# A decoder layer's FFN by two-by-two products: loads a pair ahead, half tiles, another order of products and splits, and state loads issued by SP

## The chip, the cores and the metric

The kernel runs on one core of one Trainium2 chip. The metric is the device time of one execution in microseconds (us), as the median of the runs shown. An execution's profile gives a span, from its first to its last instruction, and the granted clock of TensorE (PE). The other engines are VectorE (DVE), ScalarE (ACT), GpSimd (POOL) and SyncE (SP), which here only issues transfers.

## The reference

One inference step of one decoder layer, for 512 prompt rows and 8 sample rows (520 columns once transposed). The parts that the change touches are the second half of the FFN and the sample group's recurrent states (`step`, for 8 samples of 32 heads, 64 by 128 each):

```python
    def step(h, inp):
        st, dec = inp
        return h * dec[..., None, None] + st, h
...
x = x + g1 * mix
h2 = rmsnorm(x, norm2_w) * (1 + sc2) + sh2
gt, up = jnp.split(h2 @ w_ffn_in, 2, axis=-1)
x = x + g2 * ((jax.nn.silu(gt) * up) @ w_ffn_out)
return x, pool_new, conv_new, ssm_new.astype(ssm_prev.dtype)
```

`w_ffn_in` is 1024 x 5632: 22 column tiles of 128 for the gate, 22 for the up part. `w_ffn_out` is 2816 x 1024: 8 output columns of 128, each over 22 tiles of 128 rows. Everything is float32. Each operand is split into a rounded part (`hi`) and the rest (`lo`), and a product is three matmuls: hi by hi, hi by lo, lo by hi.

## The kernel before

**Splits.** A weight tile is loaded by SP as `raw` (three buffers, `NRAW`), cast by ACT to `hi` (L117 or L157) and subtracted by DVE to `lo` (L118 or L158). `hi` and `lo` tiles have three buffers each, so a new cast waits until PE is done with the third tile before it.

**The FFN's first half.** Tiles 0 to 2, 20 and 21 are plain (`ffn`, L1433): two columns of 48 matmuls, then Silu on ACT and a product on DVE (L1393, L1394). Tiles 3 to 19 are 17 "pairs" (`wino`, L1527): the gate's and the up part's tile of one index are taken as a two-by-two block matrix (a11, a12 from the gate tile, a21, a22 from the up tile, each four k blocks deep), and the activations as another; seven products of 12 matmuls replace eight. `sums_of_rows` (L1455) forms once the four sums of activations that the pairs need (t0 to t3, on DVE and POOL) and splits them into `tt`. For every pair POOL forms four sums of weight blocks in place in `raw` (L1511 to L1514: a22, a21, a11, a12, each needing the one before it). They and the original blocks are split into the tiles g (both halves of the gate tile), x, y and z. Seven products go to PSUM in the order g0, g1, y0, x1, y1, z, x0; ACT copies the first (L1546), and DVE adds the others into `u2`, `u4`, `va`, `vb`, `sa`, `sb` (L1545). Silu (L1558) and a product (L1562) end the pair. PSUM has four single banks for these products, so the fifth waits until the first is read out.

**Order of the work around the change.** From `ffn_act` (L1310) on PE, ACT, DVE, POOL and SP work through the program in the order in which it is written: each engine takes its next instruction and waits for what that needs. In pair j the gate's split for pair j+1 (`wino_weights`, L1485) is written after the second product, the sums and the other splits (`wino_sums`, L1500) after the seventh, and the load of pair j+2's tiles (`wino_load`, L1477) after those.

**The FFN's second half and the states.** `ffn_out` (L1615) computes six output columns of 22 k blocks; a column's weights are three units of 8, 8 and 6 k blocks. `ahead` (L170) writes, ahead of a column, the splits of its own third unit and of the first two units of the next column. At five points of each column `states_step` (L1367) takes a step of `sample_states` (L1341), 32 states in all: POOL issues the loads of state n+2 (`hs`, four buffers, L1337; a broadcast row `bb`, three buffers, L1338), multiplies `hs` by its decay (L1353), ACT forms four scaled rows (L1359), and one step later DVE adds them (L1362) and POOL issues the store to `out_ssms` (L1363). So POOL's order in step n is: load n+2, multiply n, store n-1. `last_pair` (L1654) computes the last two output columns, and `finish` normalizes and stores the result.

Of the kernel before, what the change touches and what calls it, by code (L numbers as in the profile page):

```python
# [53 lines left out]
def tile_decoder(ctx: ExitStack, tc: tile.TileContext, I: dict, O: dict):  # L54
# [1275 lines left out]
    def state_load(n):  # L1330
        if n >= 32:
            return
        g, b = state_unit(n)
# [3 lines left out]
        nc.gpsimd.dma_start(out=h, in_=I["sssm"][g, :, b : b + 2])  # L1337
        nc.gpsimd.dma_start(out=bb, in_=dbc[g, 0, b : b + 2].unsqueeze(0).broadcast_to([P, 2, P]))  # L1338
        states[n] = h, bb

    def sample_states():  # L1341
# [4 lines left out]
        before = None
        for n in range(33):
            if n < 32:
                g, b = state_unit(n)
# [3 lines left out]
                nc.gpsimd.tensor_tensor(h, h, at.unsqueeze(3).broadcast_to([P, 2, 2, P]), ALU.mult)  # L1353
                t = G["ff"].tile([P, T], F32, tag="fs", name=f"ht{n}", bufs=NFS)[:, 0:TP]
                t = t.rearrange("p (b j n) -> p b j n", b=2, j=2)
                for i in range(2):
                    for j in range(2):
                        x = xds[:, 2 * g + j, b + i : b + i + 1]
                        nc.scalar.activation(t[:, i, j], bb[:, i], AF.Identity, bias=0.0, scale=x)  # L1359
            if before:  # L1360
                pg, pb_, ph, pt = before
                nc.vector.tensor_tensor(ph, ph, pt, ALU.add)  # L1362
                nc.gpsimd.dma_start(out=O["ssms"][pg, :, pb_ : pb_ + 2], in_=ph)  # L1363
            before = (g, b, h, t)
            yield True
# [89 lines left out]
    def sums_of_rows():  # L1455
        v, p = nc.vector.tensor_tensor, nc.gpsimd.tensor_tensor
        add, minus = ALU.add, ALU.subtract
        for k in range(4):
            b = [[[hblock(n, r, c)[:, k].bitcast(F32) for c in range(2)] for r in range(2)] for n in ("hh", "hl")]
            f1, f2 = (G["ff"].tile([P, T], F32, tag="fs", name=f"ft{k}_{i}", bufs=NFS) for i in range(2))  # L1460
            t1, t2, t3, t4 = f1[:, 0:H2], f1[:, H2:T], f2[:, 0:H2], f2[:, H2:T]
            p(t3, b[0][1][1], b[0][0][1], minus)
            p(t3, t3, b[1][1][1], add)
            p(t3, t3, b[1][0][1], minus)
# [12 lines left out]
    def wino_load(j):  # L1477
        if WINO[0] <= j < WINO[1]:
            WW["raw", j] = load(I["wfi"][j]), load(I["wfi"][NF + j])

    def wino_tiles(j, kind):
        pool, bufs = (wp, 3) if kind in "gz" else (G["we"], 2 if kind == "x" else 1)
        hi, lo = (("hi", "lo") if kind in "gz" else (f"{kind}hi", f"{kind}lo"))
        WW[kind, j] = [pool.tile([P, KD, P], F32R, tag=t, name=f"w{kind}{t}{j}", bufs=bufs) for t in (hi, lo)]

    def wino_weights(j):

        if not WINO[0] <= j < WINO[1]:
            return
        if ("raw", j) not in WW:  # L1490
            wino_load(j)
        g, u = WW["raw", j]
        wino_tiles(j, "g")
        hi, lo = WW["g", j]
        nc.scalar.copy(hi, g)
        nc.vector.tensor_tensor(lo, g, hi.bitcast(F32), ALU.subtract)
        wino_tiles(j, "x")
        split(*(t[:, 0:4] for t in WW["x", j]), u[:, 4:8])

    def wino_sums(j, between=lambda: None, silu=lambda: None):  # L1500

        if not WINO[0] <= j < WINO[1]:
            silu()
            between()
            return
        g, u = WW.pop(("raw", j))
        a11, a12, a21, a22 = g[:, 0:4], g[:, 4:8], u[:, 0:4], u[:, 4:8]
        wino_tiles(j, "y")
        wino_tiles(j, "z")
        v = nc.gpsimd.tensor_tensor  # L1510
        v(a22, a21, a22, ALU.add)  # L1511
        v(a21, a11, a21, ALU.subtract)  # L1512
        v(a11, a22, a11, ALU.subtract)  # L1513
        v(a12, a12, a11, ALU.subtract)  # L1514
        cuts = [("x", 1, a22), ("y", 0, a11), ("z", 0, a12), ("y", 1, a21)]
        cuts = [(*(t[:, 4 * h : 4 * h + 4] for t in WW[n, j]), a) for n, h, a in cuts]
        for hi, lo, a in cuts[:2]:
            nc.scalar.copy(hi, a)
        silu()
        for hi, lo, a in cuts[:2]:  # L1520
            nc.vector.tensor_tensor(lo, a, hi.bitcast(F32), ALU.subtract)
        between()
        for hi, lo, a in cuts[2:]:
            split(hi, lo, a)
        wino_load(j + 1)

    def wino(j):  # L1527
        def fn():
# [7 lines left out]
            def mult(kind, half, x):  # L1536
# [9 lines left out]
            nc.scalar.copy(u2, mult("g", 0, B(0, 0)))  # L1546
            add(sa, mult("g", 1, B(1, 0)), u2)
            wino_weights(j + 1)
            add(u2, mult("y", 0, tt[1]), u2)
            add(u4, mult("x", 1, tt[0]), u2)  # L1550
            o = mult("y", 1, tt[2])
            add(vb, o, u4)
            add(va, o, u2)
            add(sb, mult("z", 0, B(1, 1)), u4)
            o = mult("x", 0, tt[3])

            def silu():
                nc.scalar.activation(s, s, AF.Silu, bias=0.0, scale=1.0)  # L1558

            def between():  # L1560
                add(va, o, va)
                nc.vector.tensor_tensor(s, f2, s, ALU.mult)  # L1562

            wino_sums(j + 1, between, silu)
            for kind in "gxyz":
# [234 lines left out]
```

## Time and profile before

| | us |
|---|---|
| runs | 1215.45, 1215.19, 1212.05 (median 1215.19) |
| the profiled execution | 1213.03 |
| its span | 1211.3 |
| PE busy in it | 1083.4 |
| mean granted PE clock | 0.958 |

A timeline row reads: start, duration, engine, line, operation, output <- inputs with their sizes, count, and in brackets the idle time of the engine before it and what ended that. A row of the waits reads: who waited for whom, us in total, times, longest. PE's rows show a matmul's whole latency; two that follow each other start one matmul's pace apart.

### The profile page before, as it was taken

How to read it: one execution, taken by the hardware profiler on the slowest of the kernel's cores; microseconds unless marked ns; L12 is line 12 of the kernel's file. 1: busy time of each engine (PE TensorE's matmuls, PEld its weight loads, DVE VectorE, ACT ScalarE, POOL GpSimd, SP SyncE). 2: the span in 40 equal slices, each digit the busy share in tenths (PEclk: the TensorE clock that was granted, in tenths of full speed). 3: DMA queues.
4: the chain of work that ended last, by engine and by line, in shares of the span. 5: the costliest groups of instructions: out<-in, count | busy, mean ns of one | idle time of the engine just before them, and what ended most of it. 6: DMA issues, size and time to landing. Idle time of an engine off the chain costs nothing.

```text
span 1211.3 us, 22506 instructions
## 1 busy us (share of the span) xinstructions
PE 1083.4 (89%) x9127; PEld 1041.0 (86%) x9127; DVE 793.2 (65%) x1226; ACT 543.5 (45%) x1003; POOL 355.2 (29%) x514
## 2 busy tenths in 40 slices
PE   7988999999999999999999996888888899666685
PEld 6987999999999999999999976787777889666675
DVE  5686787777877978966765547676676682333342
ACT  4358466556644457543433342333333363334330
POOL 1132423433343310000000142434433412445451
PEclk9998999999999999999999998999999999877787
DMA  9542554346335244544445320222122144555552
GB/s 361 192 118 90 166 175 144 101 154 191 101 118 183 86 140 161 165 140 139 158 140 203 130 105 35 71 80 95 70 79 96 71 149 128 168 157 172 175 174 80
DMA packets 58472, 165.36 MB, mean 137 GB/s; under 512 B 10881, under 2 KB 16513, under 8 KB 57601
## 3 DMA queue, kind: packets, MB, share of 16 engines
q1 hardware_dynamic: 51712, 142.96, 35.5%
q0 software_dynamic: 6656, 20.98, 5.5%
q8 instruction: 71, 1.16, 0.4%
q14 instruction: 33, 0.26, 0.1%
HBM read 151.05 MB, written 12.86 MB: 135 GB/s over the span
## 4 chain that ended last, share of the span: by engine, by line
PE 54%; DMA 15%; POOL 12%; DVE 7%; issue 6%; ACT 5%; SPq 0%; POOLq 0%; DVEq 0%; ACTq 0%
PE m L130 45%; DMA out_ssms<-hs 7%; DMA raw<-in_wfi 5%; POOL hs L1353 2%; POOL raw L1513 2%; PE b L130 2%; DMA araw<-in_wad 2%; POOL raw L1512 2%; POOL raw L1511 2%; PE b L796 1%; POOL hs L1337 1%; PE b L771 1%; POOL bb L1338 1%; PE b L798 1%; DVE wxxlo L158 1%
## 5 line engine op out<-in xcount | busy, mean ns | idle before, releaser
L130 PE MATMUL m<-hh,whi 128*128 128x260 f32 (+1 forms) x1296 | 271.9, 289 | 4.7 <-ACT v L645 3.4
L130 PE MATMUL m<-hh,wlo 128*128 128x260 f32 (+1 forms) x1296 | 265.1, 284 | 1.1 <-DVE wlo L118 1.0
L130 PE MATMUL m<-hl,whi 128*128 128x260 f32 (+1 forms) x1296 | 265.1, 284 | 0.6 <-DVE hl L158 0.2
L130 PEld LDWEIGHTS m<-hh,whi 128*128 128x128 f32 x1296 | 202.5, 190 | 11.0 <-ACT v L645 3.6
L118 DVE TENSOR_TENSOR wlo<-raw,whi 128x1024 fp32r<-128x1024 f32 (+1 forms) x132 | 163.6, 1249 | 70.3 <-ACT whi L117 69.7
L130 PEld LDWEIGHTS m<-hh,wlo 128*128 128x128 f32 x1296 | 202.4, 190 | 1.5 <-DVE wlo L118 1.5
L130 PEld LDWEIGHTS m<-hl,whi 128*128 128x128 f32 x1296 | 202.2, 190 | 1.3 <-DVE hl L158 0.8
L117 ACT CAST whi<-raw 128x1024 fp32r<-128x1024 f32 (+1 forms) x132 | 133.2, 1020 | 137.0 <-PE m L130 107.8
L653 DVE SCALAR_TENSOR_TENSOR v<-xb,cwh,v 128x512 f32<-128x512 f32 x96 | 72.0, 751 | 39.4 <-POOL xb L640 19.3
L130 PE MATMUL m<-ah,whi 128*128 128x260 f32 x264 | 58.3, 305 | 39.3 <-ACT whi L117 39.3
L342 POOL TENSOR_TENSOR r<-me,mhalf 128x5 f32<-128x5 f32 (+2 forms) x6 | 6.4, 1068 | 259.0 <-DVE me L341 259.0
L1362 DVE TENSOR_TENSOR hs<-hs,ht 128x512 f32<-128x512 f32 x32 | 22.8, 712 | 91.0 <-POOL hs L1353 90.9
L130 PEld LDWEIGHTS m<-ah,whi 128*128 128x128 f32 x264 | 45.4, 210 | 40.3 <-ACT whi L117 40.3
L1359 ACT ACTIVATE ht<-bb,xds 128x128 f32<-128x128 f32 x128 | 40.8, 390 | 68.9 <-DMA bb<-dbc 68.8
L130 PE MATMUL m<-ah,wlo 128*128 128x260 f32 x264 | 58.3, 305 | 3.5 <-DVE wlo L118 3.5
L1511 POOL TENSOR_TENSOR raw<-raw 128x512 f32<-128x512 f32 x17 | 21.8, 1285 | 126.4 <-DVE wxxlo L158 126.4
L130 PE MATMUL m<-al,whi 128*128 128x260 f32 x264 | 57.4, 302 | 0.0
L644 ACT COPY xb<-m 128x520 f32<-128x520 f32 (+1 forms) x31 | 17.9, 577 | 81.0 <-PE m L130 81.0
L130 PE MATMUL m<-gh,whi 128*128 128x260 f32 x256 | 52.8, 288 | 0.0
L130 PE MATMUL m<-gl,whi 128*128 128x260 f32 x256 | 51.3, 282 | 0.0
L130 PE MATMUL m<-gh,wlo 128*128 128x260 f32 x256 | 51.3, 282 | 0.0
L130 PEld LDWEIGHTS m<-ah,wlo 128*128 128x128 f32 x264 | 45.1, 209 | 4.9 <-DVE wlo L118 4.9
(383 smaller groups left out, 2757.3 us busy)
## 6 DMA issues: line engine op xcount, KB each, us to landing
raw<-in_win SPq DMA_DIRECT2D x73, 512.0 KB, 4.8
raw<-in_wfi SPq DMA_DIRECT2D x44, 512.0 KB, 4.1
araw<-in_wada SPq DMA_DIRECT2D x24, 512.0 KB, 4.0
h<-in_sssm SPq DMA_DIRECT2D x16, 512.0 KB, 4.2
raw<-in_wssd SPq DMA_DIRECT2D x16, 512.0 KB, 3.4
hs<-in_sssm POOLq DMA_DIRECT2D x32, 256.0 KB, 3.3
raw<-in_wfo SPq DMA_DIRECT2D x16, 512.0 KB, 5.2
out_ssms<-hs POOLq DMA_DIRECT2D x32, 256.0 KB, 2.8
```

Of the source, the lines that this page charges most:

```text
L117: nc.scalar.copy(hi, raw)
L118: nc.vector.tensor_tensor(lo, raw, hi.bitcast(F32), ALU.subtract)
L130: nc.tensor.matmul(o, a[:, k, c0 : c0 + P], b[:, t0:t1], start=f, stop=e)
L158: nc.vector.tensor_tensor(lo, src, hi.bitcast(F32), ALU.subtract)
L644: nc.scalar.copy(shape(xb[:, 3 + t0 : 3 + t1]), o)
L653: nc.vector.scalar_tensor_tensor(v[:, 0:TP], xb[:, k : k + TP], w(k), v[:, 0:TP], ALU.mult, ALU.add)
L1353: nc.gpsimd.tensor_tensor(h, h, at.unsqueeze(3).broadcast_to([P, 2, 2, P]), ALU.mult)
L1359: nc.scalar.activation(t[:, i, j], bb[:, i], AF.Identity, bias=0.0, scale=x)
L1362: nc.vector.tensor_tensor(ph, ph, pt, ALU.add)
L1511: v(a22, a21, a22, ALU.add)
L1512: v(a21, a11, a21, ALU.subtract)
L1513: v(a11, a22, a11, ALU.subtract)
```

## The change

- `sums_of_rows` stands before tile 1's `ffn` instead of after it. It works on two k blocks at a time (two rounds of 520-wide operations instead of four of 260), in buffers of `as` that are not yet in use, and the last-but-one sum (t4, two operations a round) moves from DVE to POOL.
- Loads run two pairs ahead: `wino_load(j + 2)` is written in pair j after the second product, and odd pairs put the up tile into a buffer of its own (`ur`).
- The half tiles x0, x1, y0, y1 get a rotation of five buffers. The products go in the order g0, g1, x0, y0, x1, y1, z.
- A pair begins with the next pair's first splits: x0, then POOL's sums a22 and a21; then the Silu and product left over from the pair before; then the gate tile's split and POOL's a11 and a12. The splits y0, x1, z and y1 stand between the adds of the products.
- `state_load` issues from SP. A state's add and store stand in its own step. The last two of the six columns take six steps (`STEPS`), so that no state is left over.

```diff
-        nc.gpsimd.dma_start(out=h, in_=I["sssm"][g, :, b : b + 2])
-        nc.gpsimd.dma_start(out=bb, in_=dbc[g, 0, b : b + 2].unsqueeze(0).broadcast_to([P, 2, P]))
+        nc.sync.dma_start(out=h, in_=I["sssm"][g, :, b : b + 2])
+        nc.sync.dma_start(out=bb, in_=dbc[g, 0, b : b + 2].unsqueeze(0).broadcast_to([P, 2, P]))
...
-            if before:
-                pg, pb_, ph, pt = before
-                nc.vector.tensor_tensor(ph, ph, pt, ALU.add)
-                nc.gpsimd.dma_start(out=O["ssms"][pg, :, pb_ : pb_ + 2], in_=ph)
-            before = (g, b, h, t)
+            nc.vector.tensor_tensor(h, h, t, ALU.add)
+            nc.gpsimd.dma_start(out=O["ssms"][g, :, b : b + 2], in_=h)
...
+    def wino_first(n, mult=None, silu=None):
+        if WINO[0] <= n < WINO[1]:
+            g, u = WW["raw", n]
+            a11, a12, a21, a22 = g[:, 0:4], g[:, 4:8], u[:, 0:4], u[:, 4:8]
+            split(*half_tile(n, "x0"), a22)
+            v = nc.gpsimd.tensor_tensor
+            v(a22, a21, a22, ALU.add)
+            v(a21, a11, a21, ALU.subtract)
+        if silu:
+            silu()
+            mult()
+        if WINO[0] <= n < WINO[1]:
...
+            split(hi, lo, g)
+            v(a11, a22, a11, ALU.subtract)
+            v(a12, a12, a11, ALU.subtract)
...
+            wino_first(j + 1, *G.pop("left", ()))
+            nc.scalar.copy(u2, mult("g", B(0, 0)))
+            add(sa, mult("g", B(1, 0), 1), u2)
+            wino_load(j + 2)
+            p4 = mult("x0", tt[3])
+            p6 = mult("y0", tt[1])
+            wino_cut(j + 1, "y0")
+            add(u2, p6, u2)
+            add(va, p4, u2)
+            p5 = mult("x1", tt[0])
+            wino_cut(j + 1, "x1", "z")
+            add(u4, p5, u2)
+            p7 = mult("y1", tt[2])
+            wino_cut(j + 1, "y1")
+            add(vb, p7, u4)
+            add(va, p7, va)
...
+            add(sb, mult("z", B(1, 1)), u4)
...
+    todo(sums_of_rows)
     for j in range(1, W0):
...
-        if j == 1:
-            todo(sums_of_rows)
```

On ACT, around the row sums, before: the two casts of tile 2's weights (`whi`), then tile 1's Silu, then the casts of the row sums (`t0h` and on; `ft` holds a sum).

```order
L117 CAST whi_9051<-raw_9049 128x1024
L117 CAST whi_9057<-raw_9055 128x1024
L1393 ACTIVATE as_8976<-m_9061 128x520
L157 CAST t0h<-ft_0_9161 128x260
L157 CAST t1h<-ft_0_9161 128x260
L157 CAST t3h<-ft_1_9162 128x260
```

After the change (`as_8985` and on hold the sums):

```order
L158 CAST t0h<-as_8985 128x520
L158 CAST t1h<-as_8986 128x520
L158 CAST t3h<-as_8988 128x520
L158 CAST t2h<-as_8987 128x520
L158 CAST t0h<-as_8989 128x520
L158 CAST t1h<-as_8990 128x520
L158 CAST t3h<-as_8992 128x520
L158 CAST t2h<-as_8991 128x520
L118 CAST whi_9087<-raw_9085 128x1024
L118 CAST whi_9093<-raw_9091 128x1024
```

All eight casts of row sums now stand ahead of the casts of tile 2's weights. On DVE the subtractions moved in the same way.

On DVE, one pair before, from the gate's split of the next pair to its last half tile (`wxx`, `wyy`, `wz`, `wg` are the tiles x, y, z, g; `fs` and `as` the sums of products; `b` a PSUM bank):

```order
L1496 TENSOR_TENSOR wglo_9935<-raw_9900,wghi_9934 128x1024
L158 TENSOR_TENSOR wxxlo_9939<-raw_9902,wxxhi_9938 128x512
L1545 TENSOR_TENSOR fs_0_9904<-b_9942,fs_0_9904 128x260
L1545 TENSOR_TENSOR fs_0_9904<-b_9956,fs_0_9904 128x260
L1545 TENSOR_TENSOR fs_1_9905<-b_9970,fs_0_9904 128x260 x2
L1545 TENSOR_TENSOR as_8982<-b_9985,fs_0_9904 128x260
L1521 TENSOR_TENSOR wxxlo_9939<-raw_9902,wxxhi_9938 128x512
L1521 TENSOR_TENSOR wyylo_10013<-raw_9900,wyyhi_10012 128x512
L1545 TENSOR_TENSOR fs_1_9905<-b_9999,fs_1_9905 128x260
L1562 TENSOR_TENSOR as_8982<-fs_1_9905,as_8982 128x520
L158 TENSOR_TENSOR wzlo_10015<-raw_9900,wzhi_10014 128x512
L158 TENSOR_TENSOR wyylo_10013<-raw_9902,wyyhi_10012 128x512
```

One pair after, from the first split of the next pair (`wx0el`) to the add of the sixth product (`ur` and `raw` are the loaded tiles):

```order
L159 TENSOR_TENSOR wx0el_10016<-ur_9922,wx0eh_10015 128x512
L1553 TENSOR_TENSOR as_8982<-fs_1_9879,as_8982 128x520
L159 TENSOR_TENSOR wglo_10024<-raw_9924,wghi_10023 128x1024
L1532 TENSOR_TENSOR as_8983<-b_10043,fs_0_10013 128x260
L159 TENSOR_TENSOR wy0el_10088<-raw_9924,wy0eh_10087 128x512
L1532 TENSOR_TENSOR fs_0_10013<-b_10074,fs_0_10013 128x260
L1532 TENSOR_TENSOR fs_1_10014<-b_10061,fs_0_10013 128x260
L159 TENSOR_TENSOR wx1el_10107<-ur_9922,wx1eh_10106 128x512
L159 TENSOR_TENSOR wzlo_10111<-raw_9924,wzhi_10110 128x512
L1532 TENSOR_TENSOR fs_0_10013<-b_10093,fs_0_10013 128x260
L159 TENSOR_TENSOR wy1el_10129<-ur_9922,wy1eh_10128 128x512
L1532 TENSOR_TENSOR fs_1_10014<-b_10115,fs_0_10013 128x260
```

The splits were in two groups around the adds, and now stand one or two at a time between them; the pair's closing product (L1553) stands after the next pair's x0 split.

On POOL, two steps of the states before:

```order
L1353 TENSOR_TENSOR hs_12104<-hs_12104,dtx 128x512
L1363 DMA out_ssms<-hs_12068 128x512
L1337 DMA hs_12250<-in_sssm 128x512
L1338 DMA bb_12251<-dbc 128x256
L1353 TENSOR_TENSOR hs_12178<-hs_12178,dtx 128x512
L1363 DMA out_ssms<-hs_12104 128x512
L1337 DMA hs_12286<-in_sssm 128x512
L1338 DMA bb_12287<-dbc 128x256
```

After, three steps on POOL:

```order
L1360 DMA out_ssms<-hs_11978 128x512
L1352 TENSOR_TENSOR hs_11982<-hs_11982,dtx 128x512
L1360 DMA out_ssms<-hs_11982 128x512
L1352 TENSOR_TENSOR hs_11986<-hs_11986,dtx 128x512
L1360 DMA out_ssms<-hs_11986 128x512
L1352 TENSOR_TENSOR hs_12022<-hs_12022,dtx 128x512
```

And what SP issues now between two columns (`raw` are weights of the second half):

```order
L1338 DMA hs_12130<-in_sssm 128x512
L1339 DMA bb_12131<-dbc 128x256
L109 DMA raw_12169<-in_wfo 128x1024
L109 DMA raw_12175<-in_wfo 128x768
L109 DMA raw_12177<-in_wfo 128x1024
L1338 DMA hs_12204<-in_sssm 128x512
L1339 DMA bb_12205<-dbc 128x256
L1338 DMA hs_12240<-in_sssm 128x512
L1339 DMA bb_12241<-dbc 128x256
```

POOL has a multiply and a store for each state and no load; the loads stand in SP's queue, in one order with the weight loads.

More of the change, by code (lines that the diff above doesn't have):

```diff
@@ L1457, in sums_of_rows @@
         add, minus = ALU.add, ALU.subtract
[L1458 to L1464, printed above, removed]
+        for q in range(2):
+            ks = slice(2 * q, 2 * q + 2)
+            b = [[[hblock(n, r, c)[:, ks].bitcast(F32) for c in range(2)] for r in range(2)] for n in ("hh", "hl")]
+            t1, t2, t3, t4 = (G["as"][10 + 4 * q + i].rearrange("p (k c) -> p k c", c=H2) for i in range(4))
             v(t1, b[0][0][1], b[0][0][0], minus)
@@ L1469, in sums_of_rows @@
             v(t2, t2, b[1][1][1], add)
-            v(t4, b[0][1][0], t2, minus)
-            v(t4, t4, b[1][1][0], add)
+            p(t4, b[0][1][0], t2, minus)
+            p(t4, t4, b[1][1][0], add)
+            p(t3, b[0][1][1], b[0][0][1], minus)
+            p(t3, t3, b[1][1][1], add)
+            p(t3, t3, b[1][0][1], minus)
             for i, t in enumerate((t1, t2, t4, t3)):
-                split(*(x[:, k] for x in G["tt"][(0, 1, 3, 2)[i]]), t)
+                split(*(x[:, ks] for x in G["tt"][(0, 1, 3, 2)[i]]), t)
@@ L1475, in tile_decoder @@
     WW = {}
[L1477 to L1498, printed above, removed]
@@ L1500, in wino_sums, with wino_load @@
-    def wino_sums(j, between=lambda: None, silu=lambda: None):
-        if not WINO[0] <= j < WINO[1]:
-            silu()
[L1504 to L1525, printed above, removed]
+    def wino_load(n):
+        if WINO[0] <= n < WINO[1]:
+            u = I["wfi"][NF + n]
+            if n % 2:
+                raw = G["we"].tile([P, KD, P], F32, tag="ur", name=f"ur{n}", bufs=1)
+                nc.sync.dma_start(out=raw, in_=u)
+            WW["raw", n] = load(I["wfi"][n]), raw if n % 2 else load(u)
@@ L1527, in wino, with wino_cut @@
+    def wino_cut(n, *kinds):
+        if WINO[0] <= n < WINO[1]:
+            g, u = WW["raw", n]
+            for kind in kinds:
+                src = {"x1": u[:, 4:8], "y0": g[:, 0:4], "y1": u[:, 0:4], "z": g[:, 4:8]}[kind]
+                split(*half_tile(n, kind), src)
     def wino(j):
@@ L1534, in fn, with mult @@
             B = lambda r, c: (hblock("hh", r, c), hblock("hl", r, c))
-            def mult(kind, half, x):
+            def mult(kind, x, half=0):
                 hi, lo = WW[kind, j]
@@ L1545, in fn @@
             add = lambda out, a, b: nc.vector.tensor_tensor(out, a, b, ALU.add)
[L1546 to L1565, printed above, removed]
+            wino_first(j + 1, *G.pop("left", ()))
[14 more added lines that the diff above has]
+            add(va, p7, va)
+            if j + 1 == WINO[1]:
+                ahead(len(W["made"]) + 1, 1)
+            add(sb, mult("z", B(1, 1)), u4)
+            G["left"] = (
+                lambda: nc.vector.tensor_tensor(s, f2, s, ALU.mult),
+                lambda: nc.scalar.activation(s, s, AF.Silu, bias=0.0, scale=1.0),
+            )
+            if j + 1 == WINO[1]:
+                wino_first(j + 1, *G.pop("left"))
+            for kind in ("g", "x0", "x1", "y0", "y1", "z"):
                 WW.pop((kind, j))
+            WW.pop(("raw", j))
         return fn
```

43 lines of the change are left out of this document (25 added, 18 removed).

## The prediction

> **What bounds the kernel now.** I read the page first. Its chain of work that ended last gives PE just over half of the span:
>
> ```profile
> PE 54%; DMA 15%; POOL 12%; DVE 7%; issue 6%; ACT 5%; SPq 0%; POOLq 0%; DVEq 0%; ACTq 0%
> ```
>
> The rest is waits, so the waits of PE are the next view:
>
> ```profile
> PE m L130 <- ACT whi L117: 39.9, 6, 9.5
> PE b L1542 <- DVE fs L1545: 18.3, 16, 1.2
> PE b L1542 <- DVE wyylo L1521: 12.8, 17, 0.8
> PE b L331 <- DVE acc L392: 8.9, 3, 5.9
> PE b L1542 <- ACT wyyhi L1518: 5.0, 17, 1.6
> ```
>
> They lie in three places, each with a limit of its own. The change touches them and a fourth, the row sums; the timeline shows each.
>
> *The pairs.* The Silu that closes a pair comes once a pair on ACT, and PE's matmuls follow each other like this:
>
> ```profile
> 837.85 0.28 PE L1542 MATMUL b<-hh,wghi 128*128 128x260 f32 x1
> 837.97 0.28 PE L1542 MATMUL b<-hl,wghi 128*128 128x260 f32 x1
> 838.44 0.64 ACT L1558 ACTIVATE as<-as 128x520 f32<-128x520 f32 x1
> ...
> 851.46 0.63 ACT L1558 ACTIVATE as<-as 128x520 f32<-128x520 f32 x1
> ```
>
> A pair takes 13.02 us; its 7 x 12 = 84 matmuls at 0.12 are 10.08. The 2.9 between are the waits on `fs`, `wyylo` and `wyyhi` (36.1 over 17 pairs), with what follows them.
>
> *The states.* In the second half PE's wait on `whi` comes once a column:
>
> ```profile
> 1033.00 0.51 PE L130 MATMUL m<-ah,whi 128*128 128x260 f32 x2 [3.16 <-ACT whi L117]
> ...
> 1146.24 0.80 PE L130 MATMUL m<-ah,whi 128*128 128x260 f32 x2 [9.52 <-ACT whi L117]
> ```
>
> These are the first and the last of five, four columns apart: 113.24 / 4 = 28.3 a column, though PE has 22 x 6 x 0.12 = 15.8 of work in it. One state of POOL, and who made POOL wait for its loads:
>
> ```profile
> 1050.79 0.54 POOL L1337 DMA_DIRECT2D hs<-in_sssm  x1 [3.56 <-DMA out_ssms<-hs]
> 1051.87 1.06 POOL L1353 TENSOR_TENSOR hs<-hs,dtx 128x512 f32<-128x512 f32 x1
> 1052.87 0.58 POOL L1363 DMA_DIRECT2D out_ssms<-hs  x1
>   DMA out_ssms<-hs: 82.8, 28
> ```
>
> A load reuses the buffer whose store POOL issued last (that of state n-2, in step n-1), so it waits until that has landed: 82.8 / 28 = 2.96. With two issues (1050.79 to 1051.87: 1.08), the multiply (1.00 to the next row) and the store's issue (0.58) that is 5.6 a state, and five states are 28.1, the column's 28.3. So a serial chain on POOL sets the second half.
>
> *The row sums* stand now before pair 3 and hold it up; *the last pair* has a wait of its own. Their rows are below.
>
> **The change part by part, against the profiled execution's 1213.0.**
>
> *Pairs.* Loads two ahead, the odd pairs' own buffer and the fuller rotation take away waits for buffers; they cost SP issues that nobody waits for. Once they are gone, the next limit is the four sums of POOL in each pair and DVE's subtractions. Rows of one pair:
>
> ```profile
> 846.32 1.82 DVE L1545 TENSOR_TENSOR fs<-b,fs 128x260 f32<-128x260 f32 x4
> 846.53 1.29 POOL L1511 TENSOR_TENSOR raw<-raw 128x512 f32<-128x512 f32 x1 [7.29 <-DVE wxxlo L158]
> 847.90 1.30 POOL L1512 TENSOR_TENSOR raw<-raw,raw 128x512 f32<-128x512 f32 x1
> 848.51 1.24 DVE L1521 TENSOR_TENSOR wxxlo<-raw,wxxhi 128x512 fp32r<-128x512 f32 x1
> 849.28 1.62 POOL L1513 TENSOR_TENSOR raw<-raw,raw 128x512 f32<-128x512 f32 x1
> ...
> 853.86 0.68 DVE L158 TENSOR_TENSOR wzlo<-raw,wzhi 128x512 fp32r<-128x512 f32 x1
> 854.47 0.69 DVE L158 TENSOR_TENSOR wyylo<-raw,wyyhi 128x512 fp32r<-128x512 f32 x1
> 855.07 0.42 DVE L1545 TENSOR_TENSOR as<-b,fs 128x260 f32<-128x260 f32 x1
> 855.41 1.22 DVE L1496 TENSOR_TENSOR wglo<-raw,wghi 128x1024 fp32r<-128x1024 f32 x1
> ```
>
> A subtraction that fell beside POOL took 1.24 against 0.68 alone: it got on when the sum beside it ended (847.90 + 1.30 = 849.20), and the sum issued meanwhile at 849.28 took 1.62 against 1.30. The four adds with an operand in PSUM ran beside two sums at 0.45 each and cost them nothing. So subtractions and POOL sums take turns, adds don't. The Trainium skill ("SBUF — State Buffer", "Who interferes with whom") says so as a rule: a DVE instruction with two SBUF inputs and a GpSimd one that reads SBUF exclude each other for the whole instruction. By it a pair takes the 12.4 worked out next, and without it the 11.2 of a rival below; these rows agree with the rule.
>
> In the new order the two engines make one loop per pair: split x0, POOL a22, a21, the closing product, split g, POOL a11, a12, split y0, the adds, split x1 and z, split y1 among them, and round. Four sums at 1.37 (start to start) = 5.48; five half splits and the closing product at 0.61 = 3.66; g at 1.15 (its 1.22 less the overlap of 0.07 seen between the other rows); of the seven adds six stand behind y0, in this loop, at 0.34 (855.07 to 855.41): 2.04. Sum 12.3; 12.9 if the adds go at the 0.45 measured beside POOL. I take 12.4, since none of those six stands beside POOL in this order, against PE's 10.08. So a pair gains 0.6, and PE still waits.
>
> *Row sums.* They move from after tile 1 to before it, but in ACT's and DVE's order this puts them ahead of tile 2's casts and subtractions, which ran during tile 1. The rows around it:
>
> ```profile
> 720.32 0.76 DVE L1394 TENSOR_TENSOR as<-m,as 128x256 f32<-128x256 f32 x2 [0.35 <-ACT as L1393]
> ...
> 732.08 0.49 PE L130 MATMUL m<-hh,whi 128*128 128x260 f32 x2
> ...
> 753.75 0.59 PE L1542 MATMUL b<-hh,wghi 128*128 128x260 f32 x1 [9.88 <-ACT wghi L1495]
> ...
> 853.25 0.70 DVE L1562 TENSOR_TENSOR as<-fs,as 128x520 f32<-128x520 f32 x1
> ...
> 977.97 0.50 PE L130 MATMUL m<-hh,whi 128*128 128x260 f32 x2 [0.70 <-ACT whi L117]
> ```
>
> The sums can start at about 721, behind tile 0's product (first row). A round has, in a row, five DVE operations of 520 (0.73 from the row of 0.70 with a gap: 3.65) and five of POOL (1.37, as 512 elements above: 6.9), the splits of DVE that take their turn between these (an estimate: two or three of a round's four at 0.69, 1.7), and the last cast and subtraction (1.3): 13.5. Two rounds end at 748, tile 2's cast follows (2.71 / 3 = 0.90 for 768 by a row below, so 1.2 for 1024), and PE, which started tile 2 at 732.08, starts it at about 749.2: 17 us idle. The clock granted after PE's present wait of 9.88 stands in the stretch from 754 to 757, in the third column from the end:
>
> ```profile
> 754.00:757.00 3.00, 2.54 (x11) 2.24 (x12) 1.56 (x2) 0.27 (x2) 1.29 (x2) 0.50 0.00 0
> ```
>
> Half speed for three microseconds; after the 17 it costs about 2. What it buys: tile 2's 96 matmuls (11.5) now lie after the sums instead of before, and pair 3's splits hide under them, so pair 3 starts at 749.2 + 11.5 + 2 = 762.7 rather than 753.75. With 11.5 for it (an estimate: between PE's 10.1 and the 12.4) and sixteen at 12.4, the plain tile 20 starts at 762.7 + 11.5 + 198.4 = 972.6, before at 977.97. **First half: -5** (pair at 12.3: -7; at 12.9: +3).
>
> *States.* POOL loses two issues and the wait; what is late next is either the serial turn multiply, DVE's add, store, or the ring of four buffers. Rows for both, and for the column's end:
>
> ```profile
> 1032.13 2.71 ACT L117 CAST whi<-raw 128x768 fp32r<-128x768 f32 x3
> ...
> 1057.87 0.69 DVE L1362 TENSOR_TENSOR hs<-hs,ht 128x512 f32<-128x512 f32 x1 [4.21 <-POOL hs L1353]
> ...
> 1061.02 1.76 ACT L117 CAST whi<-raw 128x768 fp32r<-128x768 f32 x2
> hs<-in_sssm POOLq DMA_DIRECT2D x32, 256.0 KB, 3.3
> out_ssms<-hs POOLq DMA_DIRECT2D x32, 256.0 KB, 2.8
> ```
>
> The turn: 1.06 + 0.69 + 0.58 and two handovers of 0.1 make 2.5, since the store now stands in its own state's step and POOL's next multiply waits behind it. The ring: store 2.8, load 3.3, then 2.5 of work, over four buffers, 2.2. I take 2.5. A column is then the three casts (2.71), five turns (12.5), the step from the last add to the next column's cast (1061.02 less the add's end at 1058.5: 2.55) and about 1.5 for state loads that now stand behind weight loads in SP's one queue (lower end 0, upper 3.3, one whole landing): 19.3, from 17.8 to 21; a six-state column 21.8. PE needs 15.8, so it still waits some 3. Three columns of five and one of six: 3 x 19.3 + 21.8 = 79.7 for 113.24, 33.5 less; half of the first wait's 3.16 as well, 1.5. **-35** (28 to 40).
>
> *Last pair.* The adds of leftover states stand before the row that PE waits for:
>
> ```profile
> 1180.20 1.01 PE L331 MATMUL b<-cst,acc 128*128 128x1 f32 x4 [5.95 <-DVE acc L392]
> ```
>
> With the two six-state columns nothing is left over: **-7**, the wait of 5.95 and a slow restart of about 1 (6 to 10).
>
> Sum: 1213.0 - 5 - 35 - 7 = 1166.0. The runs' median, 1215.2, is 2.2 above the profiled execution: **1168** (own range by the terms' ends: 1213.0 - 7 - 40 - 10 + 2.2 = 1158 to 1213.0 + 3 - 28 - 6 + 2.2 = 1184).
>
> **The rivals.** *Only the issues are saved.* The state goes on waiting 2.96 for a landed store somewhere, and loses just two issues of 0.54: 4.56 a state, 22.8 a column, 27.4 with six, so 17.4 less instead of 35: 1213.0 - 5 - 17.4 - 7 + 2.2 = 1186. For it: both kernels have four buffers, and store and load take 6.1 together. Against it: those 82.8 are POOL's waits, in its order, and POOL no longer has a load to wait with. The Trainium skill ("DMA: Bandwidth & Descriptors", "Issuing engines are not separate DMA queues") is on its side: moving a DMA to another engine saves only the time of issuing it. 0.13.
>
> *The pairs go faster than the turns allow*, if work overlaps more than the rows above show. Were the closing product and half of g's split to lie beside POOL's sums (0.61 + 0.6), a pair would take 11.2, 16 x 1.2 = 19 less: 1149. At PE's pace, 10.1, 37 less: 1131. For it, nothing of the loop is a true dependency except inside POOL's four sums; against it, the 1.24 and 1.62. 0.10 and 0.06.
>
> *Slower: SP's queue lets one state through at a time.* The load of state n+2 waits in SP for a store to land, weight loads wait behind it, and their casts stand ahead of the next states on ACT. If that closes to a ring, a state takes store, load and work in a row: 2.8 + 3.3 + 1.06 + 0.69 + 0.58 = 8.4, a column 42 (six: 50.4): 3 x 42 + 50.4 - 113.2 = 63 more: 1213.0 + 63 - 5 - 7 + 2.2 = 1266. It decides above 5.7 a state, before's own pace (6.2 with the other gains). Against it: there are four buffers, and three units of weights stay ahead. 0.05.
>
> **How the numbers follow.** Forecast 0.66, issues only 0.13, overlapping pairs 0.16, slower 0.05. The range, 1140 to 1190, holds the forecast, the issues-only case and pairs at 11.2; 1131 and 1266 are left out. About 0.3% is what a measurement of this kernel can tell from no change, here 3.6 us. Every case but the last lies lower by more; I leave 0.02 for issues only with bad pairs and a longer stop at the sums. Faster 0.93, same 0.02, slower 0.05.
>
> **What would show it.** In the changed kernel's profile: PE idle about 17 us before tile 2, and none before pair 3; Silus 12.4 apart, with subtractions or POOL sums of stretched length; no wait of POOL on a landed store, states 2.5 apart within a column, PE's waits on `whi` 19 to 22 apart; no long wait at the last pair's `acc`. Wrong would be: pairs at 10 to 11 (no exclusion), sums that end before 740, columns of 23 (issues only) or over 28 (SP's queue).

## The result and the profile after

The changed kernel takes 1159.45 us (median of 1159.38, 1160.43, 1159.51, 1158.30) against 1214.54: a ratio of 0.955 (0.953 to 0.957), 55 us less. The forecast was 1168. The profiled execution after the change is 1159.38 with a span of 1157.6, so the two spans differ by 53.7. Three instants of PE that both traces have divide it into four stretches (1.5 of the first difference lies ahead of the changed code: tile 0's product starts at 720.32 before and at 718.81 after):

| stretch | before | after | difference | forecast |
|---|---|---|---|---|
| to the start of plain tile 20 | 977.97 | 962.32 | -15.6 | -5 |
| from there to the first wait for a column's `whi` | 55.0 | 54.3 | -0.7 | -1.5 |
| from the first to the last of these waits, four columns | 113.2 | 88.4 | -24.8 | -33.5 |
| from the last of them to the end | 65.1 | 52.6 | -12.5 | -7 |

The chain of work that ended last, and the longest waits of PE, after:

```profile
PE 60%; DVE 12%; issue 9%; DMA 7%; ACT 6%; POOL 5%; SPq 1%; POOLq 0%; DVEq 0%; ACTq 0%
```

```profile
PE b L1529 <- DVE fs L1532: 24.6, 15, 1.7
PE m L131 <- ACT whi L118: 19.7, 5, 6.8
PE m L131 <- ACT as L1389: 15.9, 1, 15.9
```

The chain's DMA share has halved and POOL's has fallen from 12 to 5; DVE's has risen from 7 to 12. In PE's waits the one for `whi` is halved, a new single one of 15.9 stands before tile 2, and the pairs have one wait each, for a bank that an add must empty. The timeline at the row sums and the first and last pair:

```profile
718.81 0.76 DVE L1390 TENSOR_TENSOR as<-m,as 128x256 f32<-128x256 f32 x2 [0.77 <-ACT as L1389]
...
746.75 0.80 PE L131 MATMUL m<-hh,whi 128*128 128x260 f32 x2 [15.90 <-ACT as L1389]
...
761.02 0.28 PE L1529 MATMUL b<-hh,wghi 128*128 128x260 f32 x1
...
962.32 0.40 PE L131 MATMUL m<-hh,whi 128*128 128x260 f32 x2
```

PE stands idle before tile 2, then comes to pair 3 without a wait, as forecast. It waits not for tile 2's weights but for tile 1's Silu (L1389), which reads a PSUM tile that tile 2 needs and which stands behind the same row sums on ACT. One pair, on all three engines around it:

```profile
845.65 0.68 DVE L159 TENSOR_TENSOR wx0el<-ur,wx0eh 128x512 fp32r<-128x512 f32 x1
845.76 0.64 ACT L1554 ACTIVATE as<-as 128x520 f32<-128x520 f32 x1 [2.83 <-DVE as L1532]
846.40 1.29 POOL L1496 TENSOR_TENSOR ur<-ur 128x512 f32<-128x512 f32 x1 [5.17 <-DVE wx0el L159]
846.43 1.82 DVE L1553 TENSOR_TENSOR as<-fs,as 128x520 f32<-128x520 f32 x1
847.78 1.62 POOL L1497 TENSOR_TENSOR ur<-raw,ur 128x512 f32<-128x512 f32 x1
848.18 2.30 DVE L159 TENSOR_TENSOR wglo<-raw,wghi 128x1024 fp32r<-128x1024 f32 x1
850.62 1.31 POOL L1504 TENSOR_TENSOR raw<-ur,raw 128x512 f32<-128x512 f32 x1 [1.23 <-DVE wglo L159]
...
852.62 1.22 DVE L159 TENSOR_TENSOR wy0el<-raw,wy0eh 128x512 fp32r<-128x512 f32 x1 [1.80 <-ACT wy0eh L158]
...
857.82 0.64 ACT L1554 ACTIVATE as<-as 128x520 f32<-128x520 f32 x1 [2.83 <-DVE as L1532]
```

The Silus are 12.06 apart, against 13.02. The closing product, 0.70 alone, takes 1.82 because it gets on only when POOL's first sum ends (847.69); the split of g takes 2.30 for 1.22 because POOL's second is in the way. The two engines relay each other. Not every step of the relay is of this kind: POOL's first sum of a pair waits for x0's split and its third for g's, whose operands they overwrite, and DVE idles 1.80 before y0's split, whose tile ACT casts from POOL's third sum. These are waits for data. In the second half:

```profile
1016.61 0.80 PE L131 MATMUL m<-ah,whi 128*128 128x260 f32 x2 [3.38 <-ACT whi L118]
...
1042.72 0.58 POOL L1360 DMA_DIRECT2D out_ssms<-hs  x1 [7.64 <-DVE hs L1359]
1043.32 1.06 POOL L1352 TENSOR_TENSOR hs<-hs,dtx 128x512 f32<-128x512 f32 x1
1045.41 0.58 POOL L1360 DMA_DIRECT2D out_ssms<-hs  x1 [1.02 <-DVE hs L1359]
...
1053.43 1.28 ACT L1358 ACTIVATE ht<-bb,xds 128x128 f32<-128x128 f32 x4 [5.06 <-DMA bb<-dbc]
...
1105.04 0.80 PE L131 MATMUL m<-ah,whi 128*128 128x260 f32 x2 [6.82 <-ACT whi L118]
```

POOL's turn is 2.69 us (1042.72 to 1045.41) where it is not held up. But in this column ACT waits 5.06 for a state's broadcast row to land. The transfers, by issue, with the median to landing at the end of each row:

```profile
hs<-in_sssm SPq DMA_DIRECT2D x32, 256.0 KB, 4.7
out_ssms<-hs POOLq DMA_DIRECT2D x32, 256.0 KB, 4.4
```

They land in 4.7 and 4.4 us where they took 3.3 and 2.8 before.

### The profile page after: what moved, and what is told of

Same layout as the page of the kernel before. It is cut to its first block, busy times and chain, and to the rows that moved or that the text cites. A ratio compares the mean times of both kernels' runs of the same rounds, so it can differ in the third digit from the quotient of the medians.

```text
span 1157.6 us, 22540 instructions
## 1 busy us (share of the span) xinstructions
PE 1070.0 (92%) x9127; PEld 1037.2 (90%) x9127; DVE 809.8 (70%) x1200; ACT 539.9 (47%) x995; POOL 330.5 (29%) x448
## 3 DMA queue, kind: packets, MB, share of 16 engines
q1 hardware_dynamic: 60928, 155.54, 41.4%
q0 software_dynamic: 2560, 8.39, 1.8%
## 4 chain that ended last, share of the span: by engine, by line
PE 60%; DVE 12%; issue 9%; DMA 7%; ACT 6%; POOL 5%; SPq 1%; POOLq 0%; DVEq 0%; ACTq 0%
PE m L131 48%; PE b L131 4%; DVE wglo L159 3%; DVE fs L1532 2%; PE b L1529 2%; POOL raw L1504 2%; PE b L797 2%; DMA hs<-in_sssm 1%; POOL hs L1352 1%; DMA araw<-in_wada 1%; ACT whi L118 1%; PE b L772 1%; DMA araw<-in_wad 1%; PE b L799 1%; DMA raw<-in_win 1%
## 5 line engine op out<-in xcount | busy, mean ns | idle before, releaser
L131 PE MATMUL m<-hh,whi 128*128 128x260 f32 (+1 forms) x1296 | 273.2, 290 | 20.4 <-ACT as L1389 15.9
L119 DVE TENSOR_TENSOR wlo<-raw,whi 128x1024 fp32r<-128x1024 f32 (+1 forms) x132 | 159.5, 1215 | 65.5 <-ACT whi L118 64.8
L1352 POOL TENSOR_TENSOR hs<-hs,dtx 128x512 f32<-128x512 f32 x32 | 35.9, 1121 | 54.1 <-DMA hs<-in_sssm 53.3
L818 POOL TENSOR_TENSOR h<-h,cc 128x1024 f32<-128x1024 f32 x16 | 38.9, 2434 | 28.0 <-DMA cc<-dbc 27.0
```

Source lines behind the costliest of these rows:

```text
L119: nc.vector.tensor_tensor(lo, raw, hi.bitcast(F32), ALU.subtract)
L131: nc.tensor.matmul(o, a[:, k, c0 : c0 + P], b[:, t0:t1], start=f, stop=e)
L818: nc.gpsimd.tensor_tensor(h0, h0, cc.unsqueeze(2).broadcast_to([P, 4, 2, P]), ALU.mult)
```

## The experiments

The theory from the prediction: DVE and POOL taking turns set the pairs, POOL's serial chain set the states before the change, and the row sums' new place costs PE an idle time and pays it back. What was open after the result: which of the two edits to the states did it, why a column takes 20.8 to 24.4 instead of 19.3 to 21.8, and whether "taking turns" is more than a story. Each time stands beside runs of the kernel before on the same chip. In the profiles tile 0's product starts anywhere from 718.8 to 722.4, though all code ahead of it is the same, so distances are compared and not instants. Edits are to the changed kernel.

**Loads of states back on POOL**

```diff
-        nc.sync.dma_start(out=h, in_=I["sssm"][g, :, b : b + 2])
...
+        nc.gpsimd.dma_start(out=h, in_=I["sssm"][g, :, b : b + 2])
...
```

> The changed kernel with one edit undone: the two loads of a state are issued by POOL again; the add and the store stay in the state's own step. Theory A (it is the queue that mattered: POOL must not wait for a landed store): POOL waits again for the landing of the store of state n-2 before it can multiply state n, a state costs about 5.6 us as before the change, PE's waits in the second half stand about 28 us apart, and the time is 1159 + 4 x 7 = about 1185 to 1195. Theory B (it is the step in which the store is issued that mattered): the store of n-2 now has a whole step to land before POOL's load asks for it, POOL's wait falls from 2.96 to about 0 to 1, a state costs the two issues more (1.08) than now, 3.6 us, a column about 22 to 24, and the time is 1160 to 1172.

Measured 1176.56, ratio 0.968 (0.965 to 0.970). Who made POOL wait for its loads (before it read 82.8, 28), and two states of a column:

```profile
  DMA out_ssms<-hs: 6.2, 6
```

```profile
1058.98 0.54 POOL L1338 DMA_DIRECT2D hs<-in_sssm  x1
...
1062.73 0.54 POOL L1338 DMA_DIRECT2D hs<-in_sssm  x1
```

```profile
1021.95 0.80 PE L131 MATMUL m<-ah,whi 128*128 128x260 f32 x2 [5.56 <-ACT whi L118]
...
1119.55 0.80 PE L131 MATMUL m<-ah,whi 128*128 128x260 f32 x2 [8.73 <-ACT whi L118]
```

B's mechanism, with a larger price than B's time: the wait for landed stores is nearly gone although POOL issues the loads, a state takes 3.75, and four columns 97.6. So issuing the store in the state's own step takes 15.6 of the 113.2 by itself, and SP another 9.2 on top. The transfers land sooner than in the changed kernel, the stores in 2.8 and the loads in 3.8.

**The add and the store a step later, loads on SP**

```diff
...
-            nc.vector.tensor_tensor(h, h, t, ALU.add)
-            nc.gpsimd.dma_start(out=O["ssms"][g, :, b : b + 2], in_=h)
+            if before:
+                pg, pb_, ph, pt = before
+                nc.vector.tensor_tensor(ph, ph, pt, ALU.add)
+                nc.gpsimd.dma_start(out=O["ssms"][pg, :, pb_ : pb_ + 2], in_=ph)
+            before = (g, b, h, t)
```

> The changed kernel with the other half undone: loads stay on SP, but a state's add and store stand one step later, as before the change. Theory A (the queue alone mattered): within 3 us of the changed kernel, 1157 to 1163; POOL's turn even loses the wait for the add of its own step. Theory B (the step of the store matters, through the ring of four buffers): a buffer is held one step longer, the loads of SP wait longer for the store's landing, a state takes (4.4 + 4.7 + two steps of work) / 4, about 3.5 to 4 us instead of 2.5 to 2.9, columns of 24 to 27, and the time is 1172 to 1190.

Measured 1162.38, ratio 0.957 (0.953 to 0.960). The interval overlaps that of the changed kernel, so the two can't be told apart: A. The second and the last of the waits:

```profile
1041.29 0.80 PE L131 MATMUL m<-ah,whi 128*128 128x260 f32 x2 [9.00 <-ACT whi L118]
...
1108.88 0.80 PE L131 MATMUL m<-ah,whi 128*128 128x260 f32 x2 [9.34 <-ACT whi L118]
```

The last three columns take 67.6; in the changed kernel the same three take 67.7 (1037.38 to 1105.04). All four, counted from where PE ran out of work on the column before, take 93.1 (from 1015.77, where no wait for `whi` stands) and in the changed kernel 91.8 (from 1013.23, 3.38 before 1016.61). So the two edits are two remedies for one wait, and in these columns SP alone would have done nearly all.

**Five buffers for the states** (the fifth is a tile that is free by then)

```diff
...
+        if n % 5 < 4:
             h = sp.tile([P, 2, 2, P], F32, tag="hs", name=f"hs{n}", bufs=4)
+        else:
+            h = G["hs5"][:, 0:TP].rearrange("p (b j n) -> p b j n", b=2, j=2)
```

> The changed kernel with five buffers for the states instead of four. The columns measured 20.8 to 24.4 us where 19.3 to 21.8 were forecast. Theory C (the ring of four buffers sets the pace: in the changed kernel a store lands in 4.4 and a load in 4.7 us, (4.4 + 4.7 + 2.5) / 4 = 2.9 a state): five buffers make 2.3, under the turn of 2.5; columns of about 19 to 20, the time about 1151 to 1154. Theory D (SP's one queue: the state loads stand behind three weight loads that wait for their own buffers, some 6 us a column): nothing changes, 1157 to 1161.

Measured 1158.39, ratio 0.953 (0.951 to 0.956): no difference that can be told from the changed kernel's 0.955 (0.953 to 0.957). The four columns took 85.6 (1018.65 to 1104.26) for 88.4, and loads and stores landed later still:

```profile
hs<-in_sssm SPq DMA_DIRECT2D x32, 256.0 KB, 5.3
out_ssms<-hs POOLq DMA_DIRECT2D x32, 256.0 KB, 5.0
```

C's 1151 to 1154 is out. That one more buffer lets the loads be issued sooner and yet arrive little sooner is a reading of these two rows; no row here shows it.

**Second-half weights loaded once**

```diff
     def load(src):
+        key = same.get(id(src))
+        if key in kept:
+            return kept[key]
...
```

> The changed kernel, with the weights of the second half's first column loaded once and used for the first six columns, so that 15 of the 18 loads of these columns are left out (outputs of five columns are then formed from the first column's weights). Theory D (the state loads come late because they stand behind 1.4 MB of weights in SP's queue and on the DMA engines): loads and stores of states land in about 3 us again, ACT does not wait for them after a column's casts, columns of 17 to 19.5. Theory C (ring of four buffers, whatever else is in the queue): columns of 20 and more still.

Measured 1152.7 in one run. The waits and the transfers:

```profile
1018.59 0.80 PE L138 MATMUL m<-ah,whi 128*128 128x260 f32 x2 [2.25 <-ACT whi L125]
1037.51 0.51 PE L138 MATMUL m<-ah,whi 128*128 128x260 f32 x2 [1.29 <-ACT whi L125]
1056.44 0.51 PE L138 MATMUL m<-ah,whi 128*128 128x260 f32 x2 [0.80 <-ACT whi L125]
```

```profile
hs<-in_sssm SPq DMA_DIRECT2D x32, 256.0 KB, 4.1
out_ssms<-hs POOLq DMA_DIRECT2D x32, 256.0 KB, 3.7
```

The columns of five take 18.9 (D's 17 to 19.5) instead of 20.8 to 22.4; so 1.9 to 3.5 us of such a column come from the weights. Whether by SP's order or by the transfer engines' time this run does not separate. The column of six, 23.6 (1075.36 to 1098.95) instead of 24.4, says less: the weights of the last two columns are loaded beside it. D's "about 3 us" was too low: landings are 4.1 and 3.7.

**POOL's sums of a pair on other memory**

```diff
-            v(a22, a21, a22, ALU.add)
-            v(a21, a11, a21, ALU.subtract)
...
+            v(aw, ar[0], ar[1], ALU.add)
+            v(aw, ar[0], ar[1], ALU.subtract)
...
-            v(a11, a22, a11, ALU.subtract)
-            v(a12, a12, a11, ALU.subtract)
+            v(aw, ar[0], ar[1], ALU.subtract)
+            v(aw, ar[0], ar[1], ALU.subtract)
```

`aw` is the unused tile, and `ar` are two stretches of `t0h`.

> The four sums of POOL in each pair read and write other memory (activation sums and an unused tile), so that they take the same time but nothing waits for their data; the pairs' products are then formed from unsummed weight blocks. If DVE's subtractions and POOL's sums take turns (forecast): DVE operations beside POOL stay stretched (1.2 to 2.3 us), the two engines' occupied time is 5.5 + 3.7 + 1.15 = 10.3, and the Silus stand 10.3 to 11 us apart. If only the data mattered (a split waits for a sum, a sum for a split): no stretched operation, PE's pace, 10.1.

Measured 1146.44 in one run. POOL, no longer tied to the pairs, runs its sums one after the other. Its last, and Silus before and after it:

```profile
811.52 0.64 ACT L1555 ACTIVATE as<-as 128x520 f32<-128x520 f32 x1 [5.13 <-DVE as L1533]
823.92 0.64 ACT L1555 ACTIVATE as<-as 128x520 f32<-128x520 f32 x1 [5.13 <-DVE as L1533]
...
863.02 1.64 POOL L1506 TENSOR_TENSOR as<-t0h 128x512 f32<-128x512 f32 x1
...
879.91 0.64 ACT L1555 ACTIVATE as<-as 128x520 f32<-128x520 f32 x1 [1.36 <-DVE as L1533]
890.03 0.64 ACT L1555 ACTIVATE as<-as 128x520 f32<-128x520 f32 x1 [1.36 <-DVE as L1533]
```

This run shows the exclusion by itself. While POOL works, on data that nobody waits for, a pair takes 12.40; when POOL has run out, 10.12. No dependency between the two engines is left that could do it. The expected 10.3 to 11 for all pairs was wrong, as POOL did seven sums to a pair instead of four.

**Fills instead of sums**

```diff
-            v(a22, a21, a22, ALU.add)
-            v(a21, a11, a21, ALU.subtract)
+            v = nc.gpsimd.memset
+            for a in (a22, a22, a21, a21):
+                v(a, 0.01)
...
```

> In place of each of the four sums of POOL in a pair stand two fills of the same weight block with a constant: POOL still writes what the splits wait for, but reads nothing; the products are then of constant blocks. If it is the reading of memory by POOL that makes DVE take turns with it: no DVE operation beside a fill is stretched (the closing product 0.7, g's subtraction 1.2), and the pair loses these stretches (1.1 each) besides what a fill is shorter than a sum. If any work of POOL does it: the closing product and g's subtraction stay stretched by the fills' length.

Measured 1131.92 in one run; Silus 10.12 apart. DVE beside four fills:

```profile
854.93 2.17 POOL L1497 MEMSET ur<- 128x512 f32 x4 [5.68 <-DVE wx0el L159]
854.98 0.70 DVE L1553 TENSOR_TENSOR as<-fs,as 128x520 f32<-128x520 f32 x1
855.91 1.23 DVE L159 TENSOR_TENSOR wglo<-raw,wghi 128x1024 fp32r<-128x1024 f32 x1 [0.24 <-ACT wghi L158]
```

The product takes 0.70 and the split 1.23, both beside a busy POOL: writing alone does not hold them up. The relay's waits for data are still there in this run, with fills of 2.17 in place of two sums.

**No sums of POOL in the pairs**

```diff
-            v(a22, a21, a22, ALU.add)
-            v(a21, a11, a21, ALU.subtract)
...
-            v(a11, a22, a11, ALU.subtract)
-            v(a12, a12, a11, ALU.subtract)
```

> The four sums of POOL in each pair are left out, all else stands (the products are formed from unsummed weight blocks). If the loop of DVE and POOL sets the pair, as forecast: DVE alone has 3.7 + 1.15 + 2.4 = 7.2 us of work in a pair, so PE's 84 matmuls are the bound, Silus 10.1 us apart, 17 x 1.95 = 33 us less. If PE's banks or the loads hold the pair: 11 to 12 us still.

Measured 1130.61 in one run, Silus 10.12 apart (781.74 and 791.86): the PE bound, as expected. So POOL's sums cost the changed kernel 1.9 us in every pair.

**Row sums behind tile 1 again**

```diff
-    todo(sums_of_rows)
     for j in range(1, W0):
...
+        if j == 1:
+            todo(sums_of_rows)
```

> The changed kernel with the row sums back behind tile 1 (in their new form). Theory A (forecast: the new place idles PE before tile 2 but frees pair 3): PE starts tile 2 at about 731 instead of 746.8, but the sums' 26 us then end at about 757, pair 3's splits and POOL's sums follow, pair 3 starts at 760 and its y0 waits until 766; time 1160 to 1166, the place is worth 0 to 6 us. Rival (the place alone brought what the first half gained): pair 3 waits 10 us as before the change and more, and the time is 1170 to 1176.

Measured 1166.41, ratio 0.960 (0.958 to 0.963), 7 us above the changed kernel: just past the end of A's 1160 to 1166, and not the rival's 1170 to 1176. The idle time moves to pair 3 and is as long:

```profile
759.29 0.58 PE L1529 MATMUL b<-hh,wghi 128*128 128x260 f32 x1 [15.32 <-ACT wghi L158]
```

Pair 3 then takes 20.9 us to its Silu at 780.20, with further waits for splits and adds, where in the changed kernel it takes 12.5 (761.02 to 773.49).

**One round of row sums on each side of tile 1**

```diff
...
+        for q in rounds:
...
-    todo(sums_of_rows)
+    todo(lambda: sums_of_rows(0))
...
+        if j == 1:
+            todo(lambda: sums_of_rows(1))
```

> The changed kernel with the first round of row sums before tile 1 and the second behind it, so that tile 1's Silu and tile 2's casts stand between the two on ACT and DVE. If the 16 us of idle PE before tile 2 are only a matter of order: PE starts tile 2 at about 732, the second round runs beside tile 2 and ends at about 745, pair 3 starts at 748 instead of 761 and loses some 3 us to its y0; time 1148 to 1152. If the sums' 26 us of DVE and POOL set pair 3's start anyhow: pair 3 starts at 756 to 760, time 1155 to 1160.

Measured 1157.61, ratio 0.953 (0.950 to 0.956). PE's wait before tile 2 fell from 15.9 to 3.3:

```profile
737.45 0.51 PE L131 MATMUL m<-hh,whi 128*128 128x260 f32 x2 [3.26 <-ACT as L1389]
...
752.58 0.39 PE L1529 MATMUL b<-hh,wghi 128*128 128x260 f32 x1 [1.83 <-ACT wghi L158]
```

Twelve us of idle PE gone, and the time moved by 2: pair 3 starts early and then waits, 21.0 us to its Silu at 773.55 instead of 12.5. What sets this stretch is the relay of DVE and POOL, and PE's idle time was slack.

**Sums on DVE.** These runs suggest that a sum on POOL costs DVE up to its whole 1.3 us, where DVE does the same sum in 0.7. So: the pairs' four sums on DVE, then the row sums too, then all of it with a round on each side of tile 1 and the fifth buffer.

```diff
-            v = nc.gpsimd.tensor_tensor
+            v = nc.vector.tensor_tensor
...
-        v, p = nc.vector.tensor_tensor, nc.gpsimd.tensor_tensor
+        v = p = nc.vector.tensor_tensor
```

> The changed kernel with the four weight sums of a pair on DVE instead of POOL, all else as it stands. If DVE and POOL take turns, POOL's 1.37 of a sum is time that DVE loses, and the same sum on DVE takes 0.61 to 0.68: DVE's work in a pair is then 3.05 + 0.61 + 1.15 + 2.4 + 2.6 = 9.8 us, under PE's 10.1, and Silus stand 10.1 to 10.6 us apart: 17 x 1.5 to 1.95 = 25 to 33 less than 1159, 1126 to 1134. If POOL's sums are of use beside DVE (they run while DVE works at something else), DVE becomes the bound with 12 us or more and the time is 1159 or above.

> As the run before, and the five sums of activations in each round on DVE too. A round goes from 12.9 us to 10 sums of 0.73 and four splits of 0.7 = 10.1: PE starts tile 2 some 5.5 us sooner, 1120 to 1128. If the rounds are held by casts and splits and not by POOL: no difference from the run before.

> The version that the runs so far point to: all sums on DVE, one round of row sums on each side of tile 1, five state buffers. If the loop of sums and splits is no longer the bound, PE's idle time before tile 2 (by then about 10 us) falls to 0 to 2 and pair 3 starts some 8 us sooner: 1110 to 1120. If pair 3 still waits for its splits behind the second round: as the run before, less 1 for the fifth buffer.

| kernel | us | ratio to before |
|---|---|---|
| the change | 1159.45 | 0.955 (0.953 to 0.957) |
| pairs' sums on DVE | 1131.45 | 0.931 (0.929 to 0.933) |
| row sums too | 1121.92 | 0.923 (0.921 to 0.924) |
| with a round on each side and a fifth buffer | 1114.89 | 0.917 (0.915 to 0.919) |

One pair with its sums on DVE:

```profile
853.34 0.64 ACT L1554 ACTIVATE as<-as 128x520 f32<-128x520 f32 x1 [1.50 <-DVE as L1532]
853.94 0.69 DVE L1496 TENSOR_TENSOR ur<-ur 128x512 f32<-128x512 f32 x1
854.66 0.69 DVE L1497 TENSOR_TENSOR ur<-raw,ur 128x512 f32<-128x512 f32 x1
855.27 0.69 DVE L1553 TENSOR_TENSOR as<-fs,as 128x520 f32<-128x520 f32 x1
855.88 1.22 DVE L159 TENSOR_TENSOR wglo<-raw,wghi 128x1024 fp32r<-128x1024 f32 x1
...
863.47 0.64 ACT L1554 ACTIVATE as<-as 128x520 f32<-128x520 f32 x1 [1.52 <-DVE as L1532]
```

10.13 a pair, nothing stretched, and PE waits for nothing in the pairs. DVE shows no idle time either: both are full. All three times fell into their ranges; what the last kernel's two further edits bring each is not told apart. In the last kernel the second round still ends 2.5 us late for pair 3:

```profile
748.03 0.39 PE L1534 MATMUL b<-hh,wglo 128*128 128x260 f32 x1 [2.49 <-DVE wglo L159]
```

## Why the prediction was right, and where it was off

**Pairs: right, the exclusion shown.** Forecast 12.4 a pair by turns, measured 12.06. That DVE and POOL exclude each other is shown by the run with POOL on other memory (12.40 and 10.12) and by the fills. The Trainium skill's rule ("SBUF — State Buffer", "Who interferes with whom") held in both halves here: two inputs in SBUF against a POOL instruction that reads contend, and one that only writes does not, as the product's 0.70 and the split's 1.23 beside the fills show. The rivals that let pairs run at 11.2 or 10.1 are out for the change as it stands.

One sentence of the prediction does not hold: "nothing of the loop is a true dependency except inside POOL's four sums". The pair's rows show three more between the engines, among them the one for which DVE idles 1.80 before y0's split. So the 1.9 us over PE's pace are exclusion and waits for data together, and no run separates them fully. An estimate from the run with fills: it keeps these waits, and its fills shorten POOL's work by at most 1.1 a pair (four sums at 1.37 against twice 2.17); what else it gains, some 0.8 or more, is the exclusion's.

**First half: -15.6 for -5, the sum mis-sized.** The start was right: 749.2 forecast for tile 2 and 746.75 measured, 762.7 for pair 3 and 761.02, though before tile 2 PE waits for tile 1's Silu and not for tile 2's cast. But I charged sixteen pairs at 12.4 after an 11.5, 209.9 in all, and the seventeen took 201.3. Some 5 of that are the 0.34 of each pair. Another 3 are pair 19, behind which no pair follows that needs sums: its Silu comes at 963.34, 9.1 after that of pair 18, at 954.24. The rest are the starts, 1.5 of them from ahead of the changed code.

**States: right in kind, -24.8 for -33.5; three terms of the sum were too small.** The columns of five took 20.8, 22.4 and 21.0 for 19.3 and that of six 24.4 for 21.8. The term "about 1.5 for state loads that now stand behind weight loads" is 1.9 to 3.5, by the run without most of the weights. But the 18.9 of that run is itself 1.1 above the 17.8 that the sum gives with nothing for this term. The turn of 2.5 is 2.69, some 0.3 a column. And the step from the last add to the next column's cast, put at 2.55, takes 3.39 (1055.49 to 1058.88). It grew by one operation on 8 columns. Before the change, and after it:

```profile
1059.46 0.17 DVE L383 TENSOR_TENSOR x<-x,gat 128x8 f32<-128x8 f32 x1
```

```profile
1056.38 1.10 DVE L384 TENSOR_TENSOR x<-x,gat 128x8 f32<-128x8 f32 x1
1056.39 1.06 POOL L1352 TENSOR_TENSOR hs<-hs,dtx 128x512 f32<-128x512 f32 x1
```

Both its inputs are in SBUF, and it ends with POOL's multiply of the next state, which now starts at that moment. It takes 1.10 in each of the first five columns after the change, and 0.17 in the run with the loads back on POOL. So the pairs' exclusion costs the states 0.9 a column as well, and the prediction looked for it in the pairs alone. The first wait for `whi` did not shrink either (3.16 and 3.38), hence -0.7 for -1.5.

A step of its reasoning was only half the cause: the forecast gave the lost wait to the move to SP. The runs show that the store in its own step takes the wait away as well, without SP (97.6 for four columns against 113.2). What SP adds to that in the four columns is 9.2 for 21 states, 0.44 each, where two issues of 0.54 are 1.08. In the whole kernel it is 15.1: another 2.2 stand before the first wait and 3.7 in the end stretch. So the rival "only the issues are saved" was wrong about the change as a whole; beside the other edit, SP saves the columns less than the issues. The rival with one state at a time in SP's queue is out: no column came near 42.

**The end: -12.5 for -7.** The wait for `acc` that I counted, 5.95, is gone. The slow restart, put at about 1, is 2.0: from PE's matmul on `acc` to that on `sqlast` it is 16.8 before (1180.20 to 1197.01) and 14.8 after (1131.85 to 1146.67). The sixth column takes 1.2 less. The remaining 3.4 I had not seen at all: from the end of POOL's last product to the end of the span it is 8.75 before (1202.55 to 1211.3) and 5.39 after (1152.21 to 1157.6). Only the kernel before and the run with the state loads on POOL (8.7) have the long tail; every run with these loads on SP has 5.3 to 5.4. What fills it no view shows.

**Row sums: the move is worth 7 us** (1166.4 against 1159.45). The idle time is the same in both places, 15.9 and 15.3; what the move buys is that pair 3's splits hide under tile 2, as the prediction had it. One round on each side takes most of the idle time away and gains 2.

The errors of the first half and the end were of opposite sign to that of the states, so the total, 8.5 us off, looks better than its terms. Some sums are slightly off without moving the forecast: six adds at 0.45 make the pair 13.0 and not 12.9, a state without its issues takes 4.54 and not 4.56, and as the four columns hold 20 states before and 21 after, the pace above which the slowest rival decides is 5.4 a state and not 5.7.

## What to carry to other kernels

An engine that helps out is no help if it blocks the one that it relieves: look at the rows of both where they overlap, and if the helped engine's instructions stretch there, compare the helper's duration with what the work would cost at home. When an idle stretch of the bounding engine vanishes and the time does not, that stretch was slack of another loop; move the loop's work, not the wait. Where two edits each remove the same wait, undo them one at a time before crediting either.

## What the runs showed of the hardware

- A sum of 128x512 takes 1.29 us on POOL and 0.69 on DVE. A DVE instruction with both inputs in SBUF that is issued while POOL reads waits until that sum ends, and then POOL's next one is held in turn (1.62 for 1.29). I had expected this; that POOL on unrelated data costs each pair 2.3 us, with seven sums to a pair, I had not. Even a DVE instruction of 128x8 takes 1.10 instead of 0.17 beside POOL's multiply of 1.06.
- Adds with one operand in PSUM are not held up (0.41 at 853.25 in the run with POOL's sums on other memory, beside one of them), nor were the product and the split beside POOL's fills.
- A state's transfers of 256 KB landed in 2.8 (store) and 3.3 us (load) before, in 4.4 and 4.7 after, in 5.0 and 5.3 with a fifth buffer, in 3.7 and 4.1 without most of the weights, and in 2.8 and 3.8 with the loads back on POOL. That the landings grow because more transfers stand in the queues at once is argued from these numbers, not tried by itself. Another cause is open: by the page, the move to SP also takes the loads from the queue q0, software_dynamic (20.98 MB before, 8.39 after) to q1, hardware_dynamic (142.96 and 155.54).
